# Attention scores over 128 rows, with the causal mask set by GpSimd

## The chip, the cores and the metric

The kernel runs on one core of one Trainium2 chip. The metric is the device time of one execution in microseconds (us). Its five instruction queues are called PE (the matrix engine), DVE (the vector engine), ACT (the scalar engine), POOL (GpSimd) and SP (here only a queue of loads). Each takes its own instructions strictly in the order in which they were written for it, and waits at one whose inputs or buffers aren't ready.

## The reference, cut to what matters

A trunk of two layers over 1024 tokens of 1024 features, in float32. The change lies in one part of the first layer, its stick-breaking attention: 8 heads of 64 features, each query looking only at earlier keys.

```python
z = jnp.einsum('bhqd,bhkd->bhqk', qb, kh).astype(jnp.float32) * scale
mask = key_pos[None, :] < q_pos[:, None]
log_beta = jax.nn.log_sigmoid(z)
log_keep = jnp.where(mask, log_beta - z, 0.0)          # log(1 - beta); 0 where masked: keep = 1
log_keep_after = lax.cumsum(log_keep, axis=3, reverse=True) - log_keep
w = jnp.where(mask, jnp.exp(log_beta + log_keep_after), 0.0)
return jnp.einsum('bhqk,bhkd->bhqd', w.astype(vh.dtype), vh)
```

Beside it the first layer has an HGRN2 recurrence (4 heads of 128), then come an output projection, a squared-ReLU MLP, and a second layer with a convolution module and another MLP.

## The kernel before, in words

Everything is held with features on the 128 partitions and tokens along the free dimension, in two halves a and b of 512 tokens. A weight panel [128, 1024] is loaded by SP into `wraw` (2 buffers), and split into a high part (ACT, L99) and a low part (DVE, L100), `whl`, 3 buffers. A GEMM of a panel (L110 to L112) is 24 products of 512 columns: high by high, high by low, low by high, for 8 tiles of the contraction. Its result stays in one of two PSUM banks `mm` until DVE or ACT has taken it (`raw` at L274 and L276); a panel whose output is turned is written back into the same bank by four transposes (L281).

The attention goes by head and by half of the queries; in a half there are four blocks of 128 queries, number i of 0 to 7. `weights(i)` works on i + 1 blocks of keys, in pieces z of at most 512 columns (two PSUM banks):

- L348: the product of q (high and low parts stacked down the 128 partitions) with `kd`, the high part of k, held twice down the partitions.
- L350, only in the piece that holds the diagonal: a bfloat16 product of the identity with `negm`, which is -1e30 at and behind the diagonal. It adds the mask.
- L351: the product of q's high part with `kl`, the low part of k. Both have only 64 rows, `rows`, since an even head's `kl` lies on partitions 0 to 63 of one tile and an odd head's on 64 to 127.
- L352: ACT writes `ke`, the keep factors, as a sigmoid; L354: DVE runs a product scan backwards over the whole of `ke` (128 to 1024 columns). `ke` has 4 buffers.

Then `apply` turns two blocks of `ke` for two blocks of queries (L367, `wtr`), ACT and DVE split them into `wt` (L371, L372), and four to eight products with v add to `av` (L376). At the end of a half `ot` is formed (ACT L391, four times DVE L394) and written to `o_dram`; it comes back as `oraw` through ACT's queue (L568) and is split into `ou`, the input of the output projection. Each of that projection's panels needs `ou` of all heads.

The order of the work around this is set in two steps. `TOKENS` lists the GEMMs of the layer, and `A_SPANS` and `G_SPANS` spread the steps of the attention and HGRN heads between them; this is the order of emission. A scheduler then puts the instructions of each engine into their order at build time, from its own estimates of when inputs and buffers are ready. So a change of operations or buffers changes every engine's order. From the last turned block of the attention on, the order of all engines is the same in both kernels, as are the orders of the loads.

Of the kernel before, what the change touches and what calls it, by code (L numbers as in the profile page):

```python
# [8 lines left out]
F32 = mybir.dt.float32  # L9
# [6 lines left out]
P = 128  # L16
# [7 lines left out]
# The GEMMs of the even layer's mixer in their order of emission. Panels of w_in: v of a head pair, qk of a head, f, q, i  # L24
# and g (gate) of an HGRN head, each for half a or b of the tokens; o: panels of w_out for half a; m: panels of the
# first MLP. Between them B: loads of the second half of x, S: its norm, L: loads of the mixer's output, X: of the
# residual, N: the norm before the MLP.
# [5 lines left out]
# The places (in panels) over which an attention head's steps are spread, for half a and for half b of the queries,  # L33
# and an HGRN head's, per half.
# [7 lines left out]
GF = 8                 # w_ff1 panels per group of an MLP  # L42
XW = 2                 # x tiles loaded ahead of the second weight panel
Z_PANELS = (2, 3)      # panels that go to the attention's PSUM banks while those are free
PRIO, SPRIO = 400, 800

# columns of the packed vectors
# [6 lines left out]
def kernel(  # L54
# [22 lines left out]
    # ---------------------------------------------------------------- constants  # L77
# [11 lines left out]
    # ---------------------------------------------------------------- helpers  # L89
    def panel(src, n, hl=None):  # L90
        """A weight panel [128, n] as hi and lo float32r parts."""
# [11 lines left out]
    def gemm(ps, hl, mov, koff=0, start=True, stop=True):  # L103
        """ps[128, n] += panel^T x mov; mov: list of (hi, lo) per k tile."""
        n = len(mov)
        whi, wlo = hl
        for k in range(n):
            c = slice((k + koff) * P, (k + koff + 1) * P)
            hi, lo = mov[k]
            PE.matmul(ps, whi[:, c], hi, start=start and k == 0, stop=False)  # L110
            PE.matmul(ps, whi[:, c], lo, start=False, stop=False)  # L111
            PE.matmul(ps, wlo[:, c], hi, start=False, stop=stop and k == n - 1)  # L112

    def stats(pool, tag, src, count, eps, dst):
        """dst[128, n] = (sum over src's tiles and partitions / count + eps) ** -0.5, on all partitions."""
# [21 lines left out]
    def colsum_sq(src, w=H, order=range(KT), two=False):  # L137
        """The sum of the squares of the k tiles src(k) [128, w], as one tile or as the sum of two."""
# [12 lines left out]
    def split(t, x):  # L151
        """t = (hi, lo) of x."""
# [12 lines left out]
    def scaled(src, gcol, r):  # L165
        """(hi, lo) of src(k) * g * r, for every k tile."""
# [8 lines left out]
    # ================================================================ even layer: the mixer  # L175
# [4 lines left out]
    # panels of w_in: heads' (q, k), head pairs' v, then f, q, i, gate of the four HGRN heads  # L180
    N_QK, N_V, N_F, N_Q, N_I, N_G = 0, 8, 12, 16, 20, 24

    # the last panels still held
# [12 lines left out]
    # The first half's u is x * g alone: its inverse root mean square comes in when a panel leaves PSUM.  # L196
# [22 lines left out]
    def norm1():  # L219
        """The steps of the second half's u."""  # L220
# [4 lines left out]
    # lower bound: first row of the softmax over the three logit rows  # L225
# [7 lines left out]
    for r in range(3):  # L233
# [8 lines left out]
    # masks  # L242
    identb = wk.tile([P, P], BF16, name="identb")
    DVE.tensor_copy(identb, ident)
    negm = wk.tile([P, P], BF16, name="negm")          # [q, key]: -1e30 where key >= q
    POOL.memset(negm, 0.0)
    POOL.affine_select(negm, negm, pattern=[[-1, P]], compare_op=ALU.is_gt, fill=-1e30,
                       base=0, channel_multiplier=1)
    cmask = wk.tile([P, P], BF16, name="cmask")         # [key, q]: 1 within a block of 32 where key <= q
    POOL.memset(cmask, 1.0)  # L250
    # q - key >= 0
    POOL.affine_select(cmask, cmask, pattern=[[1, P]], compare_op=ALU.is_ge, fill=0.0,
                       base=0, channel_multiplier=-1)
    # key - 32 * block(q) >= 0
# [6 lines left out]
    def proj(n, hf, turn=False):  # L261
        """Half hf of panel n's output; [token, feature] in blocks of 128 tokens when turn."""
# [22 lines left out]
    # ---------------------------------------------------------------- stick-breaking attention  # L285
    # keep[s] = sigmoid(-z) and K[s] = prod(keep[s:]): the weight beta[s] * K[s + 1] is K[s + 1] - K[s], so that the
    # output is sum(K[s] * (v[s - 1] - v[s])) plus the v of the last key of the query's block, with K = 1 from the query on.
    # An even head's q is held as (hi, lo) down the partitions, an odd one's as (lo, hi).
    kl = wk.tile([P, T], F32R, name="kl")                     # lo of k: even head, odd head
# [21 lines left out]
    def qk_proj(hd, hf):  # L311
        assert hd < 2 or (hd // 2 - 1, 1, hd % 2) in done      # kl is free
        if hf == 0:
            kd[hd] = wk.tile([P, T], F32R, tag="kd", name="kd", bufs=3)   # hi of k, twice
# [4 lines left out]
        with tc.high_priority(offset=PRIO):  # L319
            ACT.activation(kd[hd][b, tk], ps[b], AF.Copy)  # L320
            ACT.activation(qs[hd, hf][a], ps[a], AF.Copy)
            DVE.tensor_tensor(kl[a, tk], ps[b], kd[hd][b, tk].bitcast(F32), ALU.subtract)
# [3 lines left out]
    def v_split(hd, hf):  # L326
        h = hd % 2
        t = wk.tile([P, 4, P], F32R, tag=f"vh{hf}", name="vh", bufs=2 - hf)   # [token, block, (hi, lo)]
# [6 lines left out]
    def attn(hd, hf):  # L335
        """The steps of one head's attention for the queries of half hf."""
# [4 lines left out]
        def weights(i):  # L341
            nk = (i + 1) * P
            ke = wk.tile([P, T], F32, tag="ke", name="ke", bufs=4)
            q = slice((i % 4) * P, (i % 4 + 1) * P)
            for c0 in range(0, nk, H):
# [3 lines left out]
                if c0 + w == nk:  # L349
# [553 lines left out]
```

## Time and profile before

| | us |
|---|---|
| median of 3 runs | 2331.91 |
| lowest, highest run | 2331.65, 2335.13 |
| span of the profiled execution | 2333.6 |
| PE busy in it | 2314.3 (99%) |
| DVE busy | 1506.1 (65%) |
| ACT busy | 888.8 (38%) |
| POOL busy | 49.1 (2%) |

The profiled execution's own time is known only as its span, 2333.6 us from the first instruction to the last; it lies between the lowest and the highest run. PE's busy time holds the modelled tails of its products, which overlap the next one, so small waits of PE don't show in it; what one product costs PE is the distance from its start to the start of the next.

### The profile page before, as it was taken

What the parts mean: (1) busy time and instruction counts of PE and PEld (TensorE: products, weight loads), DVE (VectorE), ACT (ScalarE), POOL (GpSimd) and SP (SyncE); (2) the same over time, 40 slices, a digit from 0 to 9 for tenths busy, and PEclk for the clock granted to TensorE, in tenths of its full rate; (3) what the DMA queues carried; (4) which work ended last, traced back from release to release, by engine and by line L of the source; (5) the groups of instructions that cost most, each with busy time, mean ns of one, the idle gap of its engine ahead of it and who ended that gap; (6) DMA issues with size and microseconds to landing.
All of it is one profiled execution on the core that took longest, in us unless ns stands there. A gap on an engine that the chain in (4) does not pass through costs nothing.

```text
span 2333.6 us, 27326 instructions
## 1 busy us (share of the span) xinstructions
PE 2314.3 (99%) x10892; PEld 1900.7 (81%) x10892; DVE 1506.1 (65%) x2157; ACT 888.8 (38%) x1338; POOL 49.1 (2%) x81
## 2 busy tenths in 40 slices
PE   8999999999999999999999999999999999999998
PEld 7878878878888888888888888888888888888888
DVE  7776669657543453469999875799997546433344
ACT  5443344434433243342423363432324534332341
POOL 1000000000000000000000000000000000000000
PEclk9999999999999999999999999999999999999999
DMA  4211112242343323233323233232322232332341
GB/s 171 75 38 54 44 55 64 88 137 71 102 134 113 100 90 99 91 94 96 100 91 100 90 96 94 91 100 92 98 95 95 91 100 93 126 97 95 95 135 46
DMA packets 67343, 217.95 MB, mean 93 GB/s; under 512 B 7696, under 2 KB 9872, under 8 KB 67216
## 3 DMA queue, kind: packets, MB, share of 16 engines
q1 hardware_dynamic: 55296, 197.16, 26.5%
q10 hardware_dynamic: 10640, 16.96, 2.2%
q0 software_dynamic: 1280, 2.10, 0.5%
q8 instruction: 85, 1.39, 0.2%
q14 instruction: 42, 0.34, 0.0%
HBM read 205.70 MB, written 8.39 MB: 92 GB/s over the span
## 4 chain that ended last, share of the span: by engine, by line
PE 98%; issue 1%; DMA 0%; DVE 0%; ACT 0%; POOL 0%; POOLq 0%; DVEq 0%; ACTq 0%
PE mm L110 27%; PE mm L112 27%; PE mm L111 27%; PE av L376 2%; PE z L351 1%; PE wtr L367 1%; PE pa L110 1%; PE pg L111 1%; PE pg L110 1%; PE pa L111 1%; PE pa L112 1%; PE pg L112 1%; PE z L348 1%; PE zs L468 1%; PE stb L133 1%
## 5 line engine op out<-in xcount | busy, mean ns | idle before, releaser
L100 DVE TENSOR_TENSOR whl<-wraw,whl 128x1024 fp32r<-128x1024 f32 x364 | 445.4, 1224 | 318.5 <-ACT whl L99 317.5
L99 ACT ACTIVATE whl<-wraw 128x1024 fp32r<-128x1024 f32 x364 | 384.7, 1057 | 677.5 <-PE mm L112 535.6
L110 PE MATMUL mm<-u,whl 128*128 128x512 f32 x1456 | 574.4, 395 | 7.1 <-ACT u L212 7.1
L111 PE MATMUL mm<-u,whl 128*128 128x512 f32 x1456 | 572.6, 393 | 0.5 <-DVE u L213 0.5
L112 PE MATMUL mm<-u,whl 128*128 128x512 f32 x1456 | 572.7, 394 | 0.0
L110 PE MATMUL mm<-hid,whl 128*128 128x512 f32 (+1 forms) x1024 | 396.8, 388 | 0.0
L111 PE MATMUL mm<-hid,whl 128*128 128x512 f32 (+1 forms) x1024 | 396.3, 387 | 0.0
L112 PE MATMUL mm<-hid,whl 128*128 128x512 f32 (+1 forms) x1024 | 396.1, 387 | 0.0
L755 DVE SCALAR_TENSOR_TENSOR y<-a,vec,y 128x512 f32<-128x512 f32 x480 | 345.0, 748 | 4.2
L110 PEld LDWEIGHTS mm<-u,whl 128*128 128x128 f32 x1456 | 273.8, 188 | 66.0 <-ACT u L212 7.1
L112 PEld LDWEIGHTS mm<-u,whl 128*128 128x128 f32 x1456 | 273.9, 188 | 57.6 <-issue 2.5
L111 PEld LDWEIGHTS mm<-u,whl 128*128 128x128 f32 x1456 | 274.0, 188 | 55.9 <-issue 1.2
L112 PEld LDWEIGHTS mm<-hid,whl 128*128 128x128 f32 x1024 | 191.9, 187 | 43.8
L111 PEld LDWEIGHTS mm<-hid,whl 128*128 128x128 f32 x1024 | 191.8, 187 | 43.7 <-issue 0.2
L110 PEld LDWEIGHTS mm<-hid,whl 128*128 128x128 f32 x1024 | 191.8, 187 | 43.5 <-issue 0.2
L656 DVE TENSOR_TENSOR ht<-ht,mm 128x512 f32<-128x512 f32 x120 | 82.5, 687 | 216.0 <-PE mm L112 215.5
L638 ACT ACTIVATE relu<-mm 128x512 f32<-128x512 f32 x128 | 76.6, 598 | 341.9 <-PE mm L112 333.3
L354 DVE TENSOR_TENSOR_SCAN ke<-ke 128x128 f32<-128x128 f32 (+5 forms) x64 | 85.9, 1350 | 19.7 <-ACT ke L352 19.5
L641 DVE TENSOR_TENSOR hid<-sqr,hid 128x512 fp32r<-128x512 f32 x128 | 87.8, 686 | 12.4 <-ACT sqr L640 12.4
L640 ACT ACTIVATE sqr<-relu 128x512 f32<-128x512 f32 x128 | 79.7, 623 | 0.0
L639 ACT ACTIVATE hid<-relu 128x512 fp32r<-128x512 f32 x128 | 79.5, 621 | 0.2
L352 ACT ACTIVATE ke<-z 128x512 f32<-128x512 f32 (+2 forms) x96 | 46.5, 490 | 56.2 <-PE z L351 44.0
(204 smaller groups left out, 2442.6 us busy)
## 6 DMA issues: line engine op xcount, KB each, us to landing
wraw<-w_ff SPq DMA_DIRECT2D x257, 512.0 KB, 3.5
wraw<-w_in SPq DMA_DIRECT2D x47, 512.0 KB, 3.6
wraw<-w_glu SPq DMA_DIRECT2D x32, 512.0 KB, 3.6
wraw<-w_out SPq DMA_DIRECT2D x16, 512.0 KB, 3.6
wraw<-w_pw SPq DMA_DIRECT2D x16, 512.0 KB, 3.5
xk<-xT SPq DMA_DIRECT2D x16, 256.0 KB, 5.4
oraw<-o_dram ACTq DMA_DIRECT2D x16, 256.0 KB, 3.0
ht<-xT ACTq DMA_DIRECT2D x16, 256.0 KB, 2.8
```

The source lines that it names most:

```text
L99: ACT.activation(hi[:, :n], raw[:, :n], AF.Copy)
L100: DVE.tensor_tensor(lo[:, :n], raw[:, :n], hi[:, :n].bitcast(F32), ALU.subtract)
L110: PE.matmul(ps, whi[:, c], hi, start=start and k == 0, stop=False)
L111: PE.matmul(ps, whi[:, c], lo, start=False, stop=False)
L112: PE.matmul(ps, wlo[:, c], hi, start=False, stop=stop and k == n - 1)
L354: DVE.tensor_tensor_scan(kr, kr, kr, 1.0, ALU.mult, ALU.min)
L638: ACT.activation(t, ps, AF.Relu)
L639: ACT.activation(hh[:, 0], t, AF.Square)
L640: ACT.activation(s, t, AF.Square)
L641: DVE.tensor_tensor(hh[:, 1], s, hh[:, 0].bitcast(F32), ALU.subtract)
L656: DVE.tensor_tensor(d, d, ps, ALU.add)
L755: DVE.scalar_tensor_tensor(y, a[:, j:j + H], w(j), y, ALU.mult, ALU.add)
```

## The change

The mask is no longer a product. After the sigmoids POOL overwrites the last 128 columns of `ke` with 1 at and behind the diagonal (`affine_select`), in place, before DVE's scan: 64 such instructions, one per block of queries and head. The bfloat16 tiles `identb` and `negm` and their product go. `kl` becomes two tiles, one for even and one for odd heads, each with its other 64 partitions set to zero once at the start; the product with the low part of k then runs over all 128 rows of q, with the zeros beside it. `ke` has 3 buffers instead of 4. The diff also blanks comments, left out here.

```diff
-    identb = wk.tile([P, P], BF16, name="identb")
-    DVE.tensor_copy(identb, ident)
-    negm = wk.tile([P, P], BF16, name="negm")          # [q, key]: -1e30 where key >= q
-    POOL.memset(negm, 0.0)
-    POOL.affine_select(negm, negm, pattern=[[-1, P]], compare_op=ALU.is_gt, fill=-1e30,
-                       base=0, channel_multiplier=1)
...
-    kl = wk.tile([P, T], F32R, name="kl")                     # lo of k: even head, odd head
+    kl = [wk.tile([P, T], F32R, name=f"kl{h}") for h in range(2)]
+    POOL.memset(kl[0][64:128].bitcast(F32), 0.0)
+    POOL.memset(kl[1][0:64].bitcast(F32), 0.0)
...
-            DVE.tensor_tensor(kl[a, tk], ps[b], kd[hd][b, tk].bitcast(F32), ALU.subtract)
+            DVE.tensor_tensor(kl[hd % 2][a, tk], ps[b], kd[hd][b, tk].bitcast(F32), ALU.subtract)
...
-            ke = wk.tile([P, T], F32, tag="ke", name="ke", bufs=4)
+            ke = wk.tile([P, T], F32, tag="ke", name="ke", bufs=3)
...
-                if c0 + w == nk:
-                    PE.matmul(z[:, w - P:w], identb, negm, start=False, stop=False, skip_group_check=True)
-                PE.matmul(z[:, :w], qs[hd, hf][rows, q], kl[rows, c0:c0 + w], start=False, stop=True)
+                PE.matmul(z[:, :w], qs[hd, hf][:, q], kl[hd % 2][:, c0:c0 + w], start=False, stop=True)
                 ACT.activation(ke[:, c0:c0 + w], z[:, :w], AF.Sigmoid, scale=-0.125)
+
+            POOL.affine_select(ke[:, nk - P:nk], ke[:, nk - P:nk], pattern=[[-1, P]], compare_op=ALU.is_gt,
+                               fill=1.0, base=0, channel_multiplier=1)
             kr = ke[:, 0:nk][:, ::-1]
             DVE.tensor_tensor_scan(kr, kr, kr, 1.0, ALU.mult, ALU.min)
```

PE at the first block of queries of the first head that is scored, before. A row is line, operation, output and inputs by the program's names with their numbers, and the output's size:

```order
L111 MATMUL mm_594<-u_137,whl_597 128x512
L348 MATMUL z_476<-kd_363,qs_364 128x128
L350 LDWEIGHTS identb_219
L350 MATMUL z_476<-negm_221,identb_219 128x128
L351 MATMUL z_476<-kl_230,qs_364 128x128
L112 MATMUL mm_594<-u_137,whl_597 128x512
```

The same place in the changed kernel:

```order
L111 MATMUL mm_598<-u_137,whl_601 128x512
L345 MATMUL z_472<-kd_359,qs_360 128x128
L346 MATMUL z_472<-kl1_224,qs_360 128x128
L112 MATMUL mm_598<-u_137,whl_601 128x512
```

The bfloat16 load and product are gone, and the second z product reads a `kl` of all 128 partitions.

Place one lies between the blocks for the second half of the queries of head 5, where the `i` panel of HGRN head 2 is turned. DVE there, before (`raw_3545` is that panel's output on its way to being turned; the scans are the L354 rows on `ke`):

```order
L354 SCALAR_TENSOR_TENSOR ke_3211<-ke_3211 128x896
L100 TENSOR_TENSOR whl_3621<-wraw_3619,whl_3621 128x1024
L394 SCALAR_TENSOR_TENSOR ot_3105<-av_2980,vl_2546,ot_3105 64x128 x4
L372 TENSOR_TENSOR wt_3180<-wtr_3176,wt_3180 128x384
L372 TENSOR_TENSOR wt_3192<-wtr_3187,wt_3192 128x512
L354 SCALAR_TENSOR_TENSOR ke_3222<-ke_3222 128x1024
L479 TENSOR_TENSOR sT_3344<-zs_3345,cmask_226 128x512
L482 TENSOR_TENSOR hq_2827<-hq_2827,tot_3327 128x512
L483 TENSOR_TENSOR hf_2688<-hf_2688,tot_3327 128x512
L439 COPY hp_3495<-hf_3319 128x32
L276 TENSOR_TENSOR raw_3545<-mm_3515,rm0_158 128x512
```

DVE at the same panel in the changed kernel (`raw_3637` is the same output; L352 is now the scan's line, L370 the split of `wt`, L392 the adds into `ot`):

```order
L352 SCALAR_TENSOR_TENSOR ke_3251<-ke_3251 128x768
L352 SCALAR_TENSOR_TENSOR ke_3299<-ke_3299 128x896
L392 SCALAR_TENSOR_TENSOR ot_3189<-av_3056,vl_2606,ot_3189 64x128 x4
L370 TENSOR_TENSOR wt_3268<-wtr_3264,wt_3268 128x384
L370 TENSOR_TENSOR wt_3280<-wtr_3275,wt_3280 128x512
L352 SCALAR_TENSOR_TENSOR ke_3312<-ke_3312 128x1024
L370 TENSOR_TENSOR wt_3292<-wtr_3287,wt_3292 128x512
L477 TENSOR_TENSOR sT_3436<-zs_3437,cmask_219 128x512
L480 TENSOR_TENSOR hq_2895<-hq_2895,tot_3419 128x512
L481 TENSOR_TENSOR hf_2748<-hf_2748,tot_3419 128x512
L437 COPY hp_3587<-hf_3411 128x32
L270 TENSOR_TENSOR raw_3637<-mm_3607,rm0_158 128x512
```

With it stand ahead of these rows, from the preceding whl row on, one more scan (`ke_3238`, 640 columns) and two splits of `wt` (384 and 512 columns). Before, a weight panel's split stood among the scans, and now none does. PE at this place, in the changed kernel, from the last product of the panel whose weights are `whl_3668`:

```order
L112 MATMUL mm_3665<-u_155,whl_3668 128x512
L345 MATMUL z_3243<-kd_2965,qs_3106 128x128
L346 MATMUL z_3243<-kl1_224,qs_3106 128x128
L374 MATMUL av_3056<-wt_3141,vh_3053 128x256
L374 MATMUL av_3056<-wt_3141,vh_3053 128x128
L345 MATMUL z_3252<-kd_2965,qs_3106 128x512
L346 MATMUL z_3252<-kl1_224,qs_3106 128x512
L365 MATMUL wtr_3166<-ident_75,ke_3157 128x128 x2
L374 MATMUL av_3056<-wt_3141,vh_3053 128x128
```

From that product on PE has 84 instructions of the attention and HGRN heads in its order, 14 of them z products, ahead of the next GEMM product; before, the longest such run from there to place two had 18.

Place two lies at the end of the w_in panels of half a's users, ahead of the first panel of the output projection. ACT there, before (`raw_4289` is the output of the last panel, `ot_3957` and `ot_4063` are the last two halves of heads that the projection waits for):

```order
L371 ACTIVATE wt_4019<-wtr_4015 128x384
L590 DMA ht_4300<-xT 128x512
L590 DMA ht_4302<-xT 128x512
L391 ACTIVATE ot_3957<-av_3856 64x512
L590 DMA ht_4304<-xT 128x512
L371 ACTIVATE wt_4044<-wtr_4040 128x384
L590 DMA ht_4306<-xT 128x512
L590 DMA ht_4308<-xT 128x512
L371 ACTIVATE wt_4056<-wtr_4051 128x512
L590 DMA ht_4310<-xT 128x512
L274 ACTIVATE raw_4289<-mm_4259 128x512
```

ACT in the changed kernel, from the same panel's output (`raw_4397`) on:

```order
L268 ACTIVATE raw_4397<-mm_4367 128x512
L135 ACTIVATE hrh_3775<-stb_3789 128x512
L347 ACTIVATE ke_4025<-z_4026 128x512
L369 ACTIVATE wt_4009<-wtr_4005 128x384
L347 ACTIVATE ke_4101<-z_4102 128x128
L306 ACTIVATE vn_3870<-mm_4367 128x512
L328 ACTIVATE vh_4470<-vn_3870 128x4x64
L560 DMA o_dram7_93<-hrh_3775 128x512
L369 ACTIVATE wt_4038<-wtr_4034 128x384
L347 ACTIVATE ke_4110<-z_4111 128x256
```

Before, the last panel's output is taken when the splits of `wt` for the last head pair are all through; now it is taken first, and the splits and two sigmoids of that pair follow it, since PE's transposes for them stand behind the whole panel. On PE the run without a GEMM product at place two has 94 instructions now and had 56.

## Rows read from the trace of the kernel before

**Rows 1.** The page: busy time of PE, DVE, ACT and POOL, share, instructions.

```profile
PE 2314.3 (99%) x10892; PEld 1900.7 (81%) x10892; DVE 1506.1 (65%) x2157; ACT 888.8 (38%) x1338; POOL 49.1 (2%) x81
```

**Rows 2.** Windows: us, busy time of each engine, PE clock, DMA share, GB/s.

```profile
0.00:350.00 350.00, 342.26 (x1796) 276.42 (x1797) 249.50 (x421) 157.47 (x276) 19.88 (x36) 1.00 0.24 73
355.00:398.00 43.00, 43.00 (x239) 35.17 (x238) 41.83 (x69) 16.45 (x29) 0.00 (x0) 1.00 0.18 56
```

**Rows 3.** Timeline of PE around masked and unmasked z products: start, length, instruction.

```profile
111.45 0.40 PE L348 MATMUL z<-kd,qs 128*128 128x512 f32 x1
...
112.20 0.44 PE L348 MATMUL z<-kd,qs 128*128 128x384 f32 x1
112.49 0.23 PE L350 MATMUL z<-negm,identb 128*128 128x128 bf16 x1
...
200.26 0.78 PE L468 MATMUL zs<-hq,hf 128*128 128x64 f32 x6
200.88 0.82 PE L367 MATMUL wtr<-ident,ke 128*128 128x128 f32 x6
...
202.71 0.39 PE L111 MATMUL mm<-u,whl 128*128 128x512 f32 x1
202.94 0.34 PE L348 MATMUL z<-kd,qs 128*128 128x384 f32 x1
203.11 0.23 PE L350 MATMUL z<-negm,identb 128*128 128x128 bf16 x1
203.27 0.44 PE L351 MATMUL z<-kl,qs 64*128 64x384 f32 x1
203.64 0.51 PE L112 MATMUL mm<-u,whl 128*128 128x512 f32 x1
203.99 0.39 PE L110 MATMUL mm<-u,whl 128*128 128x512 f32 x1
```

**Rows 4.** The instructions of line 351: lengths in ns, first and last start, forms.

```profile
L351 PE MATMUL z<-kl,qs x96: 323/467/792, 43.7 to 608.6; 64*128 64x512 f32 x48, 64*128 64x128 f32 x16, 64*128 64x256 f32 x16, 64*128 64x384 f32 x16
```

**Rows 5.** Groups by line on DVE, forms apart: busy us, mean ns, idle before.

```profile
L354 DVE TENSOR_TENSOR_SCAN ke<-ke 128x1024 f32<-128x1024 f32 x8 | 18.3, 2288 | 6.6 <-ACT ke L352 6.5
...
L372 DVE TENSOR_TENSOR wt<-wtr,wt 128x512 fp32r<-128x512 f32 x48 | 32.3, 681 | 8.1 <-ACT wt L371 7.9
...
L394 DVE SCALAR_TENSOR_TENSOR ot<-av,vl,ot 64x128 f32<-64x128 f32 x64 | 18.3, 347 | 3.7 <-ACT ot L391 3.4
...
L372 DVE TENSOR_TENSOR wt<-wtr,wt 128x384 fp32r<-128x384 f32 x32 | 17.5, 549 | 4.6 <-ACT wt L371 4.4
...
L354 DVE TENSOR_TENSOR_SCAN ke<-ke 128x128 f32<-128x128 f32 x8 | 3.3, 416 | 0.0
```

**Rows 6.** Timeline of DVE behind a long scan.

```profile
381.20 0.67 DVE L479 TENSOR_TENSOR sT<-zs,cmask 128x512 f32<-128x512 f32 x1
381.79 0.68 DVE L482 TENSOR_TENSOR hq<-hq,tot 128x512 f32<-128x512 f32 x1
```

**Rows 7.** Timeline around the first panel of the output projection, all engines.

```profile
471.93 0.40 PE L112 MATMUL mm<-u,whl 128*128 128x512 f32 x1
...
476.60 0.45 ACTq L397 DMA_DIRECT2D o_dram<-ot  x1
...
489.65 0.75 PE L110 MATMUL mm<-ou,whl 128*128 128x512 f32 x1
```

**Rows 8.** Window of the 50 us around it, columns as in rows 2.

```profile
450.00:500.00 50.00, 48.61 (x247) 38.26 (x246) 38.36 (x66) 20.88 (x39) 3.03 (x3) 0.93 0.36 115
```

**Rows 9.** POOL by line: a select of 128x128 in float32 at the start.

```profile
masks.py:199 POOL TENSOR_SCALAR_AFFINE_SELECT ident<-ident 128x128 f32<-128x128 f32 x1 | 0.3, 288 | 0.0
```

**Rows 10.** Timeline of POOL and DVE where a small POOL operation meets a panel's split.

```profile
239.58 1.23 DVE L100 TENSOR_TENSOR whl<-wraw,whl 128x1024 fp32r<-128x1024 f32 x1
...
239.75 1.96 POOL L126 TENSOR_TENSOR st_r<-st_m,nhalf 128x4 f32<-128x4 f32 x1 [27.45 <-DVE st_m L124]
...
321.90 1.01 POOL L126 TENSOR_TENSOR st_r<-st_m,nhalf 128x4 f32<-128x4 f32 x1 [45.27 <-DVE st_m L124]
```

## The prediction

> **What bounds the kernel now.** First the page: PE is busy for 99% of the span, DVE for 65% [rows 1]. What shortens PE's work shortens the time, as long as nothing else comes late. Then the windows of the stage with the attention. From 0 to 350 us DVE is busy for 249.5 of 350 us, 71%, and ACT for less. From 355 to 398 us it is busy for nearly all of 43 us, and PE is still covered in full [rows 2]: DVE just keeps up there. Third, PE's timeline, read by starts, since the lengths overlap: a GEMM product of 512 columns costs 202.94 - 202.71 = 0.23 us, and six small transposes or scores start 0.62 us after the six before them, 0.10 each [rows 3]. Last, the one place where PE visibly stands: from the last GEMM product at 471.93 to the first one of the output projection at 489.65, 17.7 us [rows 7].
>
> **What leaves PE.** Take a masked tile of 384 columns. Its three products start at 202.94, 203.11 and 203.27, the next GEMM product at 203.64, and the one behind that at 203.99 [rows 3]. So the 64-row product takes 0.37 us where the first, over 128 rows, took 0.17, and the GEMM product behind it 0.35 instead of 0.23. The whole costs 1.05 - 0.23 = 0.82 us. After the change two products of 0.17 stand there: 0.34, 0.48 saved. I take this for 48 of the 64 masked tiles. The other 16 are 128 wide, where two products will cost 0.10 each, 0.20, instead of the 0.11 that goes by columns: 0.09 less saved, 0.40. Together 48 x 0.48 + 16 x 0.40 = 29.4 us.
>
> An unmasked tile: its two products and the following 384-wide one take 112.49 - 111.45 = 1.04 us [rows 3]. Less 0.17 for the latter that is 0.87, and two undisturbed products of 512 columns take 0.46: 0.41 saved. There are 96 tiles [rows 4], 32 of them unmasked: 13.1 us. In all PE loses 42.5 us of work. If the product behind a tile isn't delayed elsewhere as here (0.12 each), it is 42.5 - 96 x 0.12 = 31; I take 42.5, since the delay stands behind both kinds of tiles.
>
> On the 64-row product the Trainium skill has two rules. "TensorEngine Tiling (Array Packing)", Key Properties, says that a change of the tiling mode drains the engine; by that the loss before and behind the product goes with it, as in the sum. "TensorE: Matmul & The Clock Gate", Why this matters for your kernels, says that a single product over few rows takes as long as one over all rows. By that alone only the bfloat16 product would be saved, 64 x 0.16 = 10 us. The starts speak for the first: 0.37 against 0.17 us.
>
> **What comes in.** Each of 64 blocks of queries gets a select on POOL between ACT's last sigmoid and DVE's scan. The nearest row is a select of the same shape at the start, 0.29 us [rows 9]. It may take more: a POOL operation of 1.01 us that starts 0.17 us into a panel's split on DVE takes 1.96 us, 0.95 more, about what the split still had to run [rows 10]. So 0.29 to 1.24 us each. I take 0.5 at the places where DVE is behind, since there a scan couldn't have begun before the running DVE operation ended; elsewhere DVE's idle 29% hides it. POOL itself has nothing near its limit: at most 64 x 1.24 = 79 us over 600 us. But it takes its orders in sequence, so `kd` copies and the power of a norm wait behind a select that waits for ACT, and DVE's weight splits behind a scan that waits for POOL; panels split ahead cover such waits for PE, 24 x 0.23 = 5.5 us each. The zeroing of `kl` lies in POOL's idle start. The third `ke` buffer binds as follows: a block's sigmoid waits until the block three before it has been transposed.
>
> **Place one.** After the last product of the panel of `whl_3668`, PE has 84 instructions without a GEMM product: 14 z products at about 0.2 us and 70 small ones at 0.10, 9.8 us. The next panel needs the PSUM bank that `raw_3637` empties, and on DVE there stand before and with it: scans of 640, 768, 896 and 1024 columns, by the rows at both ends of the line (416 ns for 128, 2288 for 1024) 1.89 us in the mean, 7.5; three splits of `wt` at 0.681 and two at 0.549, 3.1; four adds at 0.347, 1.4 [rows 5]; four full-width operations at 0.68 [rows 6], 2.7. That is 14.7 us; neighbours overlap by 0.08 (0.67 long, next start 0.59 later [rows 6]), so 13.4. It begins about 1 us after the panel (z, sigmoid, select), and after it come four transposes, ACT's copy and the steps between engines, 1.4. 15.8 us against PE's 9.8: PE stands 6 us. The chain adds waits: the last block's buffer is free only after a transposition, then two sigmoids, about 2 us of idle DVE, and four selects of 0.5. Loss: 10 us; 0 if DVE has run ahead, 13 if it comes 3 us late, which a DVE as full as in [rows 2] can.
>
> **Place two.** Before, the last halves of heads are nearly through when the last w_in panel ends. Now DVE has from that point on: scans of 128, 256, 384 and 512 columns, 3.3 us; four 384-wide and two 512-wide splits, 3.6; seven full-width operations, 4.8; eight adds, 2.8; three half-width ones at about 0.4 and small ones, 1.5. 16 us, less 30 overlaps of 0.08: 13.6. It starts with ACT's copy, 0.8 us in, and the rounds of sigmoid, select, scan, transpose and split for two pairs of blocks leave it idle for about 3 us: the last `ot` is done at 17.4. From `ot`'s write to the projection it took 489.65 - 476.60 = 13.05 us [rows 7]; that is the same now. So 17.4 + 0.5 + 13.05 = 31 us instead of 17.7, 13 more, of which about 2 come back as attention work already done. Loss: 11 us, from 0 to 16. The granted clock was 0.93 over the 50 us there [rows 8]: of its two levels, 1.2 and 2.4 GHz, PE had the lower for some 7 us (0.07 x 50 / 0.5), after the thin stretch and while it was waiting anyway. A longer wait may carry that into the GEMM, 2 to 3 us, in the 16.
>
> **The rest.** Short waits of PE where DVE is dense, above all before 100 us, and late selects: 4 us, from 0 to 13 (48 other selects at a quarter of 1.1). Sum: 2333.6 - 42.5 + 10 + 11 + 4 = 2316 for the profiled execution's span. The median of the runs is 1.7 us below that span: 2315 us. The orders are the same from the end of the attention on, so nothing is won or lost there.
>
> **Rivals.**
> - The waits don't come, because the order was planned for them: PE's saving comes out, with 5 to 12 us lost. For it: before, PE never stood in the stage but at place two, though DVE was full [rows 2]. Against it: the 84 instructions are in PE's order, and DVE's sum beside them is longer. 2295 to 2302 us.
> - The waits eat the saving. DVE was full from 355 to 398 us, so PE's gain there is worth nothing, and both places at their upper ends with the rest at 10 cost 39 us: 2327 to 2337 us.
> - Slower: POOL's selects hold DVE up. The select waits for the running DVE operation and DVE's scan for the select, so that DVE stands for 0.5 to 0.95 us at each of 64 scans, 32 to 61 us. DVE's idle 29% can hide some; from 0.27 us per scan that reach PE beside the 25 us above (64 x 0.27 = 17.5) nothing is won, and 0.35 to 0.6 make it 2337 to 2353 us. For it: the 0.95 us [rows 10]. Against it: other DVE work stands between most selects and their scans.
>   "SBUF — State Buffer", Who interferes with whom, of the Trainium skill says that a GpSimd operation that reads and a DVE operation with two inputs in SBUF exclude each other, which a scan and a panel's split are; the 1.96 us agree with it.
> - The 64-row product costs no more than a 128-row one, and the saving is 10 us, with 25 lost: 2347 us. Against it stand the starts in [rows 3].
>
> **Chances.** Forecast, 2303 to 2326: 0.56. Waits don't come: 0.12. Eaten: 0.17. POOL holds DVE up: 0.13. Rows don't matter: 0.02. About 0.2% (5 us) is what a measurement can tell from no change. Faster: 0.56 + 0.12 less a little = 0.67; same 0.17; slower 0.16. The range runs from 2299 to 2336: it holds the forecast, nearly all of the eaten case and half of the first rival, 0.8.
>
> **What would show it.** In the profile after: the z product with `kl` 0.23 us before the next start for 512 columns, and no 0.12 us behind it; a PE stretch of 15 to 20 us without GEMM after the panel of `whl_3668`, with DVE at 9 tenths in it; about 31 us between the last w_in product and the first of the projection; selects of 0.3 to 1.2 us. It is wrong if PE's timeline shows no such stretches (then 2300 or less), or if the scans wait for POOL all over the stage (then over 2335).

## The result, and the profile after

The changed kernel takes 2317.49 us (median of 4 runs, 2315.93 to 2318.05), the kernel before 2331.89 us (4 runs, 2331.65 to 2335.13). The ratio is 0.9936, with an interval from 0.9922 to 0.9950: faster by 14.4 us. Forecast were 2315 us; the profiled span is 2316.2 us, forecast were 2316.

First the page's line of busy times, after, to be held against [rows 1]: PE 27 us less, POOL 28 us more, DVE as before.

```profile
PE 2287.0 (99%) x10828; PEld 1901.5 (82%) x10828; DVE 1508.4 (65%) x2156; ACT 884.9 (38%) x1338; POOL 77.4 (3%) x145
```

PE's timeline after, start and length, at an unmasked tile of 512 columns and the masked one of 384 behind it, as in [rows 3]:

```profile
108.13 0.40 PE L345 MATMUL z<-kd,qs 128*128 128x512 f32 x1
108.36 0.39 PE L346 MATMUL z<-kl,qs 128*128 128x512 f32 x1
108.59 0.33 PE L345 MATMUL z<-kd,qs 128*128 128x384 f32 x1
108.77 0.34 PE L346 MATMUL z<-kl,qs 128*128 128x384 f32 x1
108.94 0.39 PE L112 MATMUL mm<-u,whl 128*128 128x512 f32 x1
109.17 0.40 PE L110 MATMUL mm<-u,whl 128*128 128x512 f32 x1
```

Read by starts, the product with `kl` takes 0.23 us at 512 columns and 0.17 at 384, the GEMM product behind it 0.23. The masked tile costs 0.35 us instead of 0.82.

Place one. First PE's timeline of the kernel before, where the same panel ends; then that of the changed kernel, all engines:

```profile
388.52 0.39 PE L111 MATMUL mm<-u,whl 128*128 128x512 f32 x1
...
391.13 0.48 PE L112 MATMUL mm<-u,whl 128*128 128x512 f32 x1
```

```profile
353.26 0.39 PE L112 MATMUL mm<-u,whl 128*128 128x512 f32 x1
...
354.78 1.23 DVE L100 TENSOR_TENSOR whl<-wraw,whl 128x1024 fp32r<-128x1024 f32 x1 [1.88 <-ACT whl L99]
354.98 1.18 POOL L349 TENSOR_SCALAR_AFFINE_SELECT ke<-ke 128x128 f32<-128x128 f32 x1 [3.82 <-ACT ke L347]
...
356.19 1.49 DVE L352 TENSOR_TENSOR_SCAN ke<-ke 128x640 f32<-128x640 f32 x1 [0.18 <-POOL ke L349]
...
365.30 1.09 ACT L347 ACTIVATE ke<-z 128x512 f32<-128x512 f32 x2 [3.40 <-PE wtr L365]
...
366.45 0.29 POOL L349 TENSOR_SCALAR_AFFINE_SELECT ke<-ke 128x128 f32<-128x128 f32 x1 [8.08 <-ACT ke L347]
366.78 2.29 DVE L352 TENSOR_TENSOR_SCAN ke<-ke 128x1024 f32<-128x1024 f32 x1 [2.10 <-POOL ke L349]
...
371.46 0.69 DVE L270 TENSOR_TENSOR raw<-mm,rm 128x512 f32<-128x512 f32 x1
371.50 1.97 PE L466 MATMUL zs<-hq,hf 128*128 128x64 f32 x8
...
373.26 1.06 PE L275 MATMUL mm<-ident,raw 128*128 128x128 f32 x4
...
375.68 0.53 PE L110 MATMUL mm<-u,whl 128*128 128x512 f32 x1
```

A stretch of 22.4 us without a GEMM product stands where there were 2.6. The last block's sigmoids start only at 365.30, when a transposition has given a buffer free; the select waits for them and the scan, 2.10 us, for the select. The panel leaves PSUM (`raw`) at 371.46, and then come eight scores of an HGRN head on PE, the transposes (L275) and copies.

Place two, the timeline after, as in [rows 7]; ACTq is ACT's issue of DMAs:

```profile
448.19 0.39 PE L112 MATMUL mm<-u,whl 128*128 128x512 f32 x1
...
466.34 0.45 ACTq L395 DMA_DIRECT2D o_dram<-ot  x1
...
468.84 0.33 ACTq L566 DMA_DIRECT2D oraw<-o_dram  x1
...
472.86 0.48 PE L110 MATMUL mm<-ou,whl 128*128 128x512 f32 x1
```

24.7 us lie between the last w_in product and the projection, instead of 17.7. The last `ot` is written 18.1 us after that product, and the projection begins 6.5 us behind the write.

The windows of both places; columns as in [rows 2]:

```profile
353.00:376.00 23.00, 18.46 (x96) 15.67 (x95) 18.89 (x27) 10.47 (x21) 3.12 (x5) 0.78 0.10 31
448.00:473.00 25.00, 21.57 (x122) 19.02 (x121) 18.59 (x36) 13.43 (x29) 2.81 (x7) 0.80 0.46 148
```

PE is thin in both places and its granted clock, the last but two columns, falls to 0.78 and 0.80: of the two levels, 1.2 and 2.4 GHz, it had the lower for some 10 us in each, (1 - 0.78) x 23 / 0.5 and (1 - 0.80) x 25 / 0.5. DVE is busy for 18.89 of 23 us in place one, 82%: it too waits.

Where the gain came and went is seen by counting GEMM products (mm from `u` or `ou`; in each trace the last products of the attention stand behind the 1680th). "z saved" is how much less the z products took up to there: for every z product the distance to the next start (distances over 0.75 us, which are waits, left out), and for a single product of another kind behind it what that took beyond 0.23 us per 512 columns. "Lost" is z saved less gain.

| product | start before | start after | gain | z saved | lost |
|---|---|---|---|---|---|
| 901st | 366.2 | 335.1 | 31.0 | 28.8 | -2.2 |
| 961st, behind place one | 391.4 | 375.7 | 15.8 | 27.9 | 12.1 |
| 1141st | 452.1 | 432.2 | 19.9 | 30.6 | 10.7 |
| 1201st, behind place two | 489.7 | 472.9 | 16.8 | 35.9 | 19.1 |
| 1261st | 506.3 | 491.0 | 15.3 | 35.5 | 20.2 |
| 1861st | 713.9 | 696.7 | 17.2 | 37.0 | 19.8 |

The z products save 37.0 us. From the 901st to the 961st product 14.3 us are lost, from the 1141st to the 1261st 9.5, and elsewhere nothing: there the sum is -4.0. What is left, 17.2 us, is the difference of the spans, 2333.6 - 2316.2 = 17.4.

### The profile page after: what moved, and what is told of

Read it like the earlier page. It is cut to its first block, busy times and chain, and to the rows that moved or that the text cites. A ratio compares the mean times of both kernels' runs of the same rounds, so it can differ in the third digit from the quotient of the medians.

```text
span 2316.2 us, 27425 instructions
## 1 busy us (share of the span) xinstructions
PE 2287.0 (99%) x10828; PEld 1901.5 (82%) x10828; DVE 1508.4 (65%) x2156; ACT 884.9 (38%) x1338; POOL 77.4 (3%) x145
## 4 chain that ended last, share of the span: by engine, by line
PE 93%; issue 3%; DVE 2%; DMA 1%; POOL 0%; ACT 0%; POOLq 0%; DVEq 0%; ACTq 0%
PE mm L110 26%; PE mm L111 26%; PE mm L112 26%; PE av L374 1%; PE pa L110 1%; PE pg L111 1%; PE pg L110 1%; PE pa L111 1%; PE pa L112 1%; PE pg L112 1%; PE wtr L365 1%; PE zs L466 1%; PE stb L133 1%; PE st L121 1%; PE z L345 1%
## 5 line engine op out<-in xcount | busy, mean ns | idle before, releaser
L352 DVE TENSOR_TENSOR_SCAN ke<-ke 128x128 f32<-128x128 f32 (+5 forms) x64 | 86.3, 1352 | 23.6 <-POOL ke L349 23.0
L639 DVE TENSOR_TENSOR hid<-sqr,hid 128x512 fp32r<-128x512 f32 x128 | 87.9, 687 | 12.4 <-ACT sqr L638 12.4
L374 PE MATMUL av<-wt,vh 128*128 128x256 f32 (+1 forms) x320 | 63.0, 295 | 4.5 <-DVE wt L370 3.7
```

What stands on the lines that cost most here:

```text
L352: DVE.tensor_tensor_scan(kr, kr, kr, 1.0, ALU.mult, ALU.min)
L374: PE.matmul(live["av"][:, qo + o:qo + 256], vh[hd, (b0 + b) // 4][:, (b0 + b) % 4, :], wt[:, part, b * 256:b * 256 + 256 - o], start=start ...
L639: DVE.tensor_tensor(hh[:, 1], s, hh[:, 0].bitcast(F32), ALU.subtract)
```

## The experiments

There are two theories of the 20 us that are lost. A: the third `ke` buffer (in place of the fourth) makes the long runs without GEMM, by the order that is written with it and by sigmoids that wait for a buffer. B: the select does, since every scan now has POOL ahead of it. The saving may come from the rows of the `kl` product or from the bfloat16 product that went.

| run | us, median | ratio to before, interval | place one, us | place two, us | sum of z |
|---|---|---|---|---|---|
| before | 2331.89 | 1 | 2.6 | 17.7 | 76.7 |
| after | 2317.49 | 0.9936, 0.9922 to 0.9950 | 22.4 | 24.7 | 39.8 |
| e1 | 2345.94 | 1.0057, 1.0044 to 1.0070 | 18.4 | 24.8 | 78.0 |
| e2 | 2315.39 | 0.9925, 0.9913 to 0.9936 | 19.4 | 19.7 | 45.7 |
| e3 | 2348.27 | 1.0061, 1.0047 to 1.0074 | 14.9 | 32.8 | 76.1 |
| e4 | 2347.94 | 1.0067, 1.0055 to 1.0079 | 23.4 | 28.6 | 73.6 |
| e5 | 2309.32 | 0.9890, 0.9876 to 0.9903 | 4.1 | 22.0 | 44.9 |
| e6 | 2311.69 | 0.9902, 0.9888 to 0.9915 | 9.4 | 24.2 | |
| e7 | 2316.54 | 0.9920, 0.9908 to 0.9933 | 24.2 | 26.4 | |
| e8 | 2323.06 | 0.9947, 0.9933 to 0.9960 | 27.3 | 29.3 | |
| e9 | 2308.30 | 0.9894, 0.9878 to 0.9911 | 4.1 | 18.4 | |
| e10 | 2307.18 | 0.9889, 0.9874 to 0.9904 | 4.1 | 18.8 | |

A place is the distance from the start of the last GEMM product to that of the next; "sum of z" the distances of all z products and the delay behind them, as above. The runs of before beside e1 to e4 had a median of 2331.68, those beside e5 to e8 2335.39, those beside e9 and e10 2332.55; so between runs of different groups a difference of 3 or 4 us is not certain.

**e1, three buffers alone** (the kernel before):

```diff
-            ke = wk.tile([P, T], F32, tag="ke", name="ke", bufs=4)
+            ke = wk.tile([P, T], F32, tag="ke", name="ke", bufs=3)
```

> The kernel before with 3 buffers of the keep factors instead of 4, nothing else. Theory A (fewer buffers make the order bunch the attention work at the two places): the runs without a GEMM product at both places appear here too (73 and 80 instructions in PE's order), PE stands some 5 us at place one and 5 us more at place two: 2340 to 2346 us. Theory B (POOL's select lengthens the chain and makes the waits): no select, no new waits: 2330 to 2334 us.

14.3 us slower, with both runs without GEMM, though there is no select and PE is no faster. The timeline of e1 in place one:

```profile
377.99 0.39 PE L112 MATMUL mm<-u,whl 128*128 128x512 f32 x1
...
386.98 1.05 PE L367 MATMUL wtr<-ident,ke 128*128 128x128 f32 x4
...
387.86 1.09 ACT L352 ACTIVATE ke<-z 128x512 f32<-128x512 f32 x2 [2.82 <-PE wtr L367]
...
388.98 2.29 DVE L354 TENSOR_TENSOR_SCAN ke<-ke 128x1024 f32<-128x1024 f32 x1 [2.13 <-ACT ke L352]
...
396.39 0.48 PE L110 MATMUL mm<-u,whl 128*128 128x512 f32 x1
```

The same chain as after the change, without POOL: transposition, sigmoids, and a scan that waits 2.13 us. The waits of ACT's sigmoids for PE's transposes show it over the whole run: us in all, times, longest. Before, then after, then e1:

```profile
ACT ke L352 <- PE wtr L367: 8.8, 3, 3.4
```

```profile
ACT ke L347 <- PE wtr L365: 18.5, 9, 4.3
```

```profile
ACT ke L352 <- PE wtr L367: 24.2, 9, 7.0
```

Three times in the kernel before, nine in both kernels with three buffers. Theory A stands. PE's order changed along with the waits, and how much of the 14.3 us is order and how much wait, no run separates.

**e2, the change without the select** (`identb`, `negm` and their product put back):

```diff
+                if c0 + w == nk:
+                    PE.matmul(z[:, w - P:w], identb, negm, start=False, stop=False, skip_group_check=True)
...
-            POOL.affine_select(ke[:, nk - P:nk], ke[:, nk - P:nk], pattern=[[-1, P]], compare_op=ALU.is_gt,
-                               fill=1.0, base=0, channel_multiplier=1)
```

> The changed kernel with the mask as the bfloat16 product again: 128 rows of zeros beside the low part of k, 3 buffers, no select. PE saves 33.6 us of the 42.5 (0.32 for each of 64 masked tiles, 13.1 for the others). Theory A: the waits of the changed kernel are there all the same, 20 to 25 us: 2318 to 2324 us. Theory B: they are gone: 2298 to 2304 us.

2.1 us faster than the changed kernel, at the edge of what the runs tell apart, and 2.6 us below the range of theory A. Both places are there all the same, 19.4 and 19.7 us, and theory B's 2298 to 2304 us are far off. From e1 it differs by the rows of the `kl` product alone, and PE's order up to the end of the attention is the same: 30.5 us. The masked tile in e2:

```profile
107.10 0.33 PE L351 MATMUL z<-kd,qs 128*128 128x384 f32 x1
107.28 0.23 PE L353 MATMUL z<-negm,identb 128*128 128x128 bf16 x1
107.31 0.42 PE L354 MATMUL z<-kl,qs 128*128 128x384 f32 x1
107.58 0.39 PE L111 MATMUL mm<-u,whl 128*128 128x512 f32 x1
107.81 0.39 PE L112 MATMUL mm<-u,whl 128*128 128x512 f32 x1
```

Ahead of a 128-row product the mask product takes 0.03 us, not 0.16 as in [rows 3], and the product behind it 0.27 instead of 0.17. So most of the 0.16 belonged to the 64-row product behind it, and what the mask product costs by itself, 0.13, falls mostly on the next one.

**e3, the select alone** (the kernel before, 64 rows, four buffers, `identb`, `negm` and their product out):

```diff
-                if c0 + w == nk:
-                    PE.matmul(z[:, w - P:w], identb, negm, start=False, stop=False, skip_group_check=True)
...
+            POOL.affine_select(ke[:, nk - P:nk], ke[:, nk - P:nk], pattern=[[-1, P]], compare_op=ALU.is_gt,
+                               fill=1.0, base=0, channel_multiplier=1)
```

> The kernel before with the mask by POOL's select, 64 rows and 4 buffers as before. PE saves the bfloat16 product, 64 x 0.16 = 10 us, and no more. Theory A (buffers): waits of about 5 us, 2325 to 2329 us. Theory B (select): the waits of the changed kernel, 20 to 25 us: 2342 to 2348 us.

16.6 us slower by the medians, 14 by the ratio (the six runs lie between 2339.63 and 2349.99 us): about theory B's number, and A's failed. With four buffers the order is bunched too, most at place two: 32.8 us, with 126 PE products in the trace where the kernel before has 74. So both theories hold. The scans' waits for POOL are 21.0 us in 24 places, where the kernel before has 19.5 us in 13 for ACT; this speaks for a price that is mainly one of order, but no run has the select in an unchanged order. And the product that left saves less than 10 us. The sum of z goes from 76.7 to 76.1 only, but 20 z products of e3 ran while the granted clock was at its lower level, and 7 of the kernel before. With these priced like the others of their kind in the same trace, an estimate, it goes from 74.8 to 69.7. Where part of the rest stays, a masked tile of e3 shows:

```profile
469.63 0.42 PE L343 MATMUL z<-kd,qs 128*128 128x384 f32 x1
469.99 0.43 PE L344 MATMUL z<-kl,qs 64*128 64x384 f32 x1
470.35 0.45 PE L372 MATMUL av<-wt,vh 128*128 128x256 f32 x2
```

The `kd` product of 384 columns took 0.17 us ahead of the mask product in [rows 3], and takes 0.36 ahead of the 64-row one (in the median of 14 tiles each, 0.26 and 0.35): part of the delay has only moved to it.

**e4, select and three buffers, 64 rows** (the changed kernel with the product's rows put back):

```diff
-                PE.matmul(z[:, :w], qs[hd, hf][:, q], kl[hd % 2][:, c0:c0 + w], start=False, stop=True)
+                PE.matmul(z[:, :w], qs[hd, hf][rows, q], kl[rows, c0:c0 + w], start=False, stop=True)
```

> The changed kernel with the product of the low part of k over 64 rows again: select and 3 buffers. It prices the rows by themselves: against the changed kernel PE does 0.32 us more in 64 masked tiles and 13.1 us in the others, 33.6 us. Sum of the terms: 2351 us if all of it comes out. If DVE is the bound at the two places, some of it doesn't matter there: 2343 to 2349 us. If the 64 rows cost nothing: 2317 us.

As slow as e3: beside the select the third buffer costs nothing more, beside the third buffer the select only 2.0 us. The two don't add. To the changed kernel it is again 30.4 us for the rows alone.

**e5, 128 rows, mask product, four buffers of unequal size.** A block needs no more columns than its keys, so instead of three buffers of 1024 columns block i gets one of 640 + 128 x (i mod 4). Beside this, `identb`, `negm` and their product are in, the select is out, as in e2, and two small tiles of the softmax share the space of others:

```diff
-            ke = wk.tile([P, T], F32, tag="ke", name="ke", bufs=3)
+            ke = wk.tile([P, 640 + 128 * (i % 4)], F32, tag=f"ke{i % 4}", name="ke")
```

> 128 rows, the mask as the bfloat16 product, and the keep factors in four buffers of 640, 768, 896 and 1024 columns, one for each block number of a half, so that four fit. PE's order has no run without a GEMM at place one any more, and one of 107 instructions at place two. Theory A (buffers): the waits at place one are gone, those at place two stay, some 8 us beyond the kernel before: 2331.7 - 30 + 8, 2305 to 2312 us. If place one's waits come from DVE's load whatever the buffers: 2315 us as with 3 buffers, or more.

Place one has shrunk to 4.1 us. By the medians e5 is 6.1 us faster than e2, from which it differs by the buffers and the two small tiles alone, and 8.2 us faster than the changed kernel, which has the select besides. Windows of e5: the attention's second part, place two, and what follows it:

```profile
330.00:442.00 112.00, 111.46 (x625) 95.73 (x625) 89.90 (x160) 48.13 (x85) 5.59 (x7) 1.00 0.25 75
442.50:464.50 22.00, 18.68 (x137) 16.00 (x135) 20.25 (x37) 13.40 (x28) 0.00 (x0) 1.00 0.54 168
464.50:475.00 10.50, 8.67 (x34) 6.86 (x35) 6.62 (x10) 2.57 (x3) 1.94 (x1) 0.84 0.39 120
```

PE is covered through the 112 us. The clock stays at the upper level there and in place two; it falls behind that place, to 0.84 in the mean of 10.5 us. The waits of sigmoids for transposes are 8.6 us in all.

**e6, the select with those buffers**, the piece with the diagonal first and its select right behind its sigmoid:

```diff
-            for c0 in range(0, nk, H):
+            for c0 in reversed(range(0, nk, H)):
...
+                if c0 + w == nk:
+                    POOL.affine_select(ke[:, nk - P:nk], ke[:, nk - P:nk], pattern=[[-1, P]],
+                                       compare_op=ALU.is_gt, fill=1.0, base=0, channel_multiplier=1)
```

> The changed kernel (128 rows, select) with the same four buffers, and the piece with the diagonal done first in a block of over 512 keys, so that its select runs beside the sigmoid of the other piece. If buffers and the select's place in the chain are what costs: PE saves 35 us or more and waits some 10 us at place two: 2304 to 2312 us, not slower than the run with the bfloat16 product and these buffers. If the select costs by what it does to DVE and the order: 2313 to 2320 us.

Within the range that was expected, but 2.4 us slower than e5 where "not slower" was expected: a place one of 9.4 us comes with the select again.

**e7, the same reversal with three buffers.** 

> The changed kernel with the piece with the diagonal done first, 3 buffers as they are. It takes the select out of the chain for half of the blocks (32 of 64). If the select's delay of the scan costs: 3 to 8 us less than the changed kernel, 2309 to 2314 us. If the order decides (the runs without a GEMM are 100 and 96 instructions instead of 84 and 94): 2317 to 2324 us.

0.9 us from the changed kernel, no difference, and half a microsecond below the range of the theory of order. An earlier select takes nothing from the two places, though PE's order is another one too; the place in the chain isn't what costs there. e6 and e7 differ by the buffers alone: 4.9 us.

**e8, each select twice.** 

> The changed kernel with every select done twice, which changes no value. Each block's scan comes at least 0.3 us later, 0.45 by the mean length of a select. If a select's time reaches PE one to one: 64 x 0.45 = 29 us more, 2346 us. If it does so only at the two places, where about 16 selects stand: 5 to 8 us more, 2322 to 2326 us. If it is hidden: 2316 to 2319 us.

5.6 us slower than the changed kernel, both places about 5 us longer. 64 more selects on POOL, 25.9 us of busy time, cost a fifth of it, as was expected if they count only at the two places. PE's order changed as well: in the trace 108 and 136 products stand in the places, in the changed kernel 92 and 118. POOL in e8 in place one:

```profile
366.96 0.29 POOL L349 TENSOR_SCALAR_AFFINE_SELECT ke<-ke 128x128 f32<-128x128 f32 x1 [7.00 <-ACT ke L347]
367.32 0.29 POOL L352 TENSOR_SCALAR_AFFINE_SELECT ke<-ke 128x128 f32<-128x128 f32 x1
```

A second one costs 0.36 us here. At 64 scans that would be 23 us, were it on the path everywhere.

**e9 and e10, e5 with the last two heads begun earlier**, for place two (e9 has 47.5 and 48.7 as the second numbers):

```diff
-    (35, 36.5, 36.5, 36.7), (47, 48.5, 52, 66.5), (48.5, 48.7, 63, 74.5)
+    (35, 36.5, 36.5, 36.7), (46, 47, 52, 66.5), (47, 48, 63, 74.5)
```

> The best version so far (128 rows, bfloat16 mask, four buffers by block number) with heads 6 and 7 started about a panel earlier for half a: spans 46 to 47.5 and 47 to 48.7 instead of 47 to 48.5 and 48.5 to 48.7. The run without a GEMM at place two shrinks from 107 to 70 instructions. If the waits there come from attention work left behind the last panel: 4 to 8 us less, 2301 to 2306 us. If the way of the last output through memory sets that place: 2307 to 2310 us.

> The same with spans 46 to 47 and 47 to 48: the last steps of both heads still a little earlier. The run at place two has 70 instructions here too. Same two theories: 2300 to 2305 us, or 2307 to 2310 us.

Place two shrinks by 3 to 4 us, but the ratios, 0.9894 and 0.9889, don't differ from e5's 0.9890: the 2301 to 2306 us that were expected didn't come. The timeline of e10 says what comes next:

```profile
444.87 0.39 PE L112 MATMUL mm<-u,whl 128*128 128x512 f32 x1
...
454.35 0.45 ACTq L401 DMA_DIRECT2D o_dram<-ot  x1
...
459.27 0.33 ACTq L572 DMA_DIRECT2D oraw<-o_dram  x1
...
463.67 0.48 PE L110 MATMUL mm<-ou,whl 128*128 128x512 f32 x1
```

The last `ot` is written 9.5 us after the last w_in product, where e5 takes 14.8 and the changed kernel 18.1. But its reload is issued 4.9 us behind the write (3.1 in e5, 2.5 in the changed kernel), and the projection starts 4.4 us later. The way through memory and what follows it, 9.3 us, is now as long as the attention's rest. Taking it away was not tried. e10 has the lowest median, 1.1% below the kernel before, but isn't clearly faster than e5.

Taken together by medians, the three parts of the change are: a buffer less, +14.3 us (before to e1); the rows, -30.5 (e1 to e2); the select in place of the mask product, +2.1 (e2 to after). On this path the gain comes from the rows alone.

## Why the prediction was right, point by point

The time came out within 2.5 us, and the mechanism is the one that was forecast: PE loses work, and part of that is lost again at the two places. That the number is so near is luck. Two errors of about 5 us cancel in it: 37.0 us saved instead of 42.5, and 19.8 lost instead of 10 + 11 + 4 = 25; and within the 19.8 place one lost more and the rest less than forecast. Of the signs, the `kl` product and the length of most selects came as named; the stretch at place one is longer than 15 to 20 us, DVE is busy for 82% of it and not for 9 tenths, and place two has 24.7 us and not 31.

- **What leaves PE, 42.5.** The side of before came out: 48 x 0.82 + 16 x 0.60 + 32 x 0.87 = 76.8 by the forecast's prices, 76.7 measured, though 2.0 of these are an estimate of what seven products lost at the lower clock. After, the forecast has 48 x 0.34 + 16 x 0.20 + 32 x 0.46 = 34.2, the trace 39.8. Some 3 us of that lie in 31 z products within the two places, about half of it in the eight of place two that ran at the lower clock (465.8 to 470.6 us); the forecast priced every product at the upper level. The z products of place one all stand before the clock fell there. The rest is not separated.
- **The bfloat16 product, 10 by itself.** This part failed. By sums of z it is worth 5.9 us with 128 rows (e2 to after), 4.4 (e1 to e4) and 0.6 (before to e3) with 64; with the clock taken out as in e3, an estimate, 5.8, 3.3 and 5.1. The rest of what the forecast read off its starts was the delay ahead of the 64-row product, which falls on whatever stands there. In the sum of both parts this made no error, since both went together.
- **The rows.** 30.5 and 30.4 us in time, 32.3 and 33.8 in sums of z, against 29.4 + 13.1 - 10 = 32.5 (29.6 and 32.1 by the same estimate). The rival by which 64 rows cost no more than 128 is refuted. The delay of 0.13 us (e2 against [rows 3]) or 0.19 us (e3) ahead of a 64-row product and the 0.12 behind it [rows 3] are gone with 128 rows. The Trainium skill says in "TensorEngine Tiling (Array Packing)", Key Properties, that a change of the tiling mode drains the engine; these delays agree with it.
- **The selects, 0.29 to 1.24 us.** 0.28 to 1.62, 0.29 in the median and 0.45 in the mean. The first line gives the mean, the second the shortest, the median and the longest, in ns:

```profile
L349 POOL TENSOR_SCALAR_AFFINE_SELECT ke<-ke 128x128 f32<-128x128 f32 x64 | 28.7, 449 | 343.9 <-ACT ke L347 339.5 <-DVE dv L298 4.4
L349 POOL TENSOR_SCALAR_AFFINE_SELECT ke<-ke x64: 282/293/1620, 45.3 to 594.1; 128x128 f32<-128x128 f32 x64
```

  The one of 1.18 us at 354.98 runs beside a panel's split on DVE and ends 0.15 us behind it; in [rows 10] the longer POOL operation ended 0.90 us behind its split. The one of 1.62 us, at 64.12, begins 0.02 us into an operation of DVE, runs on through the scan that follows it and ends 0.09 us behind that: the forecast's upper bound allowed for one DVE operation only. The rival in which POOL holds DVE up all over the stage fell: DVE's scans wait 23.0 us for it in 21 places, little more than the 19.5 us for ACT before, and e8 shows that another select at every scan is hidden at most of them.
- **Place one, loss 10 (0 to 13).** The stretch was forecast at 15.8 + 4 = 20 us and is 22.4. Beyond the 9.8 us that the forecast gave to PE's own work, and the panel's last product, 12.4 us are left; the 14.3 by products also hold attention work that was brought into the stretch. The place, the panel, DVE's work and the waits for a buffer (2.10 us of DVE) were right: `raw` was done 18.9 us into the stretch, forecast were 1 + 13.4 + 4 = 18.4. What comes behind `raw` took 3.5 us instead of 1.4. There PE had work of its own ahead of the transposes, the eight scores of 1.97 us, and the clock was at its lower level (0.50 from 365.6 to 375.7 us), which the sum left out. What made the run was not asked: e1 shows that the third buffer alone makes one, e3 that the select alone does too.
- **Place two, loss 11 (0 to 16).** Forecast were 31 us, measured are 24.7; by products 8.4 are lost up to the projection and 9.5 with its start. `ot` was done at 18.1 (forecast 17.4). The tail is the step that failed: "that is the same now" put 13.05 us behind the write, and it was 6.5. The two halves of it both shrank. From the write to the issue of the reload it was 5.2 us before and is 2.5 now; the last load of `xT` on the same queue was issued 3.0 us ahead of the write before, and 5.1 us ahead of it now, but no run changes that alone. From the reload to the projection it was 7.8 and is 4.0. There PE still had z products of its own to do before, and at the lower clock, as this piece of its timeline shows:

```profile
477.02 0.50 PE L348 MATMUL z<-kd,qs 128*128 128x512 f32 x1
477.46 0.50 PE L351 MATMUL z<-kl,qs 64*128 64x512 f32 x1
...
481.82 0.33 ACTq L568 DMA_DIRECT2D oraw<-o_dram  x1
...
483.46 0.79 PE L348 MATMUL z<-kd,qs 128*128 128x512 f32 x1
484.18 0.79 PE L351 MATMUL z<-kl,qs 64*128 64x512 f32 x1
484.90 0.79 PE L348 MATMUL z<-kd,qs 128*128 128x512 f32 x1
```

  It is 0.72 us from start to start at 512 columns, where the first pair took 0.44 and 0.42. So the prediction's reading that PE had the lower clock "while it was waiting anyway" was wrong: PE was working. After the change PE has the same kind of work in its order ahead of the projection, but all over 128 rows and partly at the upper clock. A tail that holds other work than the transfer isn't a constant.
- **The rest, 4 (0 to 13).** 19.8 - 14.3 - 9.5 = -4.0: nothing was lost beside the two places, and the -4.0 is probably work that was brought into them.
- **Span and median.** By spans the gain was 17.4 us, as summed; by medians 14.4. A run of the changed kernel takes 1.7 us more than its span (2317.94 and 2316.2 for the profiled one); the forecast put it 1.7 below, as the median of before stood to a span of its slower end. Span plus 1.7 would have been 2318.

## What to carry to other kernels

A product over half the rows can cost more than one over all of them with zeros, and its price sits in the neighbours too: compare the starts with and without it before an instruction beside it is put down as costly. A buffer less changes the order that is written at build time as well as the waits; to find the cause of a new gap, change the number of buffers alone. Give each size of a rotating tile the buffer that it needs: here four unequal buffers instead of three full ones took back 6.1 us with the mask product (e2 to e5) and 4.9 with the select (e7 to e6).

## What the runs showed of the hardware that was not expected

- The bfloat16 product takes 0.16 us ahead of a 64-row product [rows 3] and 0.03 ahead of a 128-row one (e2). With it gone, the `kd` product of 384 columns ahead takes 0.35 us in the median (e3), where it took 0.26 before.
- The granted clock fell in stretches in which PE had little to do, 0.78 and 0.80 in the two places after, but it stayed at 1.00 in e5's 22.0 us at place two, with PE busy for 18.68 of them, and fell only behind them (0.84 in the next 10.5 us); in the changed kernel's 23 us at place one PE was busy for 18.46.
- A select, 0.29 us in the median, took 1.18 us beside a panel's split on DVE and ended 0.15 us behind it; the longest, 1.62 us, ended 0.09 us behind a scan. In e8 64 more selects cost 5.6 us, and the two places were 4.9 and 4.6 us longer.
- From the write of the last `ot` to the issue of its reload it took 5.2 us before, 2.5 after, and 4.9 in e10.
